# First mixer of a hybrid two-layer backbone: a fixed TensorE order for its products and recurrences

## The chip, the cores and the metric

The kernel runs on one core of a Trainium2 chip. The metric is the device time of one execution in microseconds. Before the change the median of three runs is 1795.73 us (1795.3 to 1796.77).

## The reference, cut to what matters

Two layers work on 512 latent tokens and 256 context tokens of width 1024, in float32. Layer 0 is the part that the change rewrites. One projection feeds two head groups: gated linear attention (GLA), a recurrence run in both directions, and softmax attention with grouped heads.

```python
gq, gk, gv, gog, gz, aq, ak, av = _split(h @ w_in, EVEN_SIZES)   # 256 256 512 512 32 512 128 128
for d, z in enumerate(jnp.split(gz, 2, axis=-1)):
    logit = (z @ gla_w_gate[d] + gla_b_gate[d])
    g = _heads(jax.nn.log_sigmoid(logit) / GLA_GATE_TAU, GLA_HEADS)
    dirs.append(_directional_scan(q, k, v, g, n_ctx, reverse=(d == 1)))   # context first, latent starts from its end state
a_lat = _gated_readout(dirs[0][1] + dirs[1][1], og[:, :, n_ctx:], gla_out_norm)   # rms(o) * silu(og)
...
o = scores(q, k, decay) @ v + (q * exp(G)) @ s       # one chunk of the recurrence
s = s * exp(G_last) + (k * exp(G_last - G)).T @ v
```

Then softmax attention over context and latent keys, one output projection, and a SwiGLU FFN. Layer 1 has a recurrence of the same form (HGRN2) and another FFN. Shift, scale and gate of every sub-layer come from a condition vector: `silu(c) @ mod_w`, 1024 x 6144 per layer.

## The kernel before, in words

**Products.** A float32 product is made of three passes with operands split into a high part `H` and a rest `L` (`mm3`, L476). `unit` (L461) loads 512 KB of weights on SP's queue into one of three `raw` buffers. ACT writes the high part `wH`, VectorE the rest `wL` (four buffers each). `gemm_nat` (L501) gives 256 output columns for all 768 tokens: three token pairs (4, 0, 2) of 48 matmuls each, in a `nat` tile of PSUM that ACT evacuates after each pair. `gemm_T` (L483) gives 128 output rows for all tokens, in a 512 and a 256 token group (tile `gqk`).

**The first mixer** (`even_mixer`, L809) needs these products: the gate input `z` (288 columns, with part of the attention queries), queries `q` and keys/values `kv` of attention, and for each of two head pairs `c`: `qk` (two `gemm_T`), values `v` and output gate `g`. The string on L909 is the order in which they are traced. `g1` is handed to `attention` as filler instead.

**The gates** (`gla_gates`, L937) come right after `z`: eight small `logit` products, two directions times two token ranges times two head pairs. All eight use one PSUM bank (`sc1`). ACT (L950) and VectorE (L953) both read it before the next can start. These eight stand ahead of all other products in trace order.

**A recurrence job** (`gla_job`, L959, and `scan`, L655) exists for each head pair and token range: `c0`, `l0`, `c1`, `l1` (context, latent; pairs 0 and 1). The latent job needs the end states of the context job. A job doubles the block size from 1 to 64 in seven levels. Each level has two ACT copies (L718), two VectorE products on `arr` (L723), and a small one (L724). In between, TensorE computes small score blocks: `pcg` after the first three and after all levels, then `pbg`. Then come the transposed keys `knpg`, the state sums `pdg`, a chain of state updates on VectorE (L789), and outputs `pog` (L796 to L806): per token tile one matmul with the scores (128 rows) and up to two with the states (64 rows, one head's half of the partitions). Two heads share a job, so `hpp` is 2. In layer 1 `hpp` is 1.

**Condition sums.** `mod_vec` (L313) multiplies 512 KB pieces of `mod_w` by one element per partition and adds them on VectorE (`macc`, L333 and L335). At the end come eight matmuls (`mod_acc`), a copy and transposes (`mod_cols`, L275), and for gates a further transpose (`gate_rows`, L371). It is a generator; `even_mixer` advances it five steps after each product. All of it ends before the first recurrence job, because its pool makes room for theirs.

**What sets the order.** Tile's planner orders each engine's instructions itself; in the first mixer it is free to. `pin` (L158) takes that away where `self.pinned` is set: each pinned matmul or transpose is queued behind whatever was traced just before it on TensorE. Until now only the second mixer sets it (L1293). Nothing else is pinned: VectorE, ACT and the DMA queues keep the planner's order. The line that a pinned instruction adds:

```python
def pin(self, r):
    if self.pinned:
        self.tc.keep_in_program_order(r)
    return r
```

**Attention preparation** (`att_prep`, L997) normalizes and rotates queries and keys, six token tiles one after another: a square on ACT, a reduction, a power on GpSimd, a product with `rs` on VectorE (L1029), and the rotation on VectorE. `attention` (L1040) turns keys and queries, then computes scores `S`, probabilities and values with a head start of three items.

Of the kernel before, what the change touches and what calls it, by code (L numbers as in the profile page):

```python
# [133 lines left out]
class Net:  # L134
# [140 lines left out]
    def mod_cols(self, l, acc, n, outs):  # L275

        nc = self.nc
        rows = self.wp.tile([P, WU], F32, tag="mraw", bufs=2, name="modrows")[:, :n]
        nc.vector.tensor_copy(rows, acc)
        pt = self.tr_tile("modT")  # L280
        nb = n // P
        for b in range(nb):
            last = self.tr(pt[:, b * P : (b + 1) * P], rows[:, b * P : (b + 1) * P], self.ident)
        v = pt[:, :n].rearrange("p (b j s) -> p j b s", b=nb, j=4)
        for m, r, k, j, row, nj in outs:
            kk = nb * nj
            bias = self.modb[:, l * 48 + 8 * m + k : l * 48 + 8 * m + k + kk]
            dst = self.modcol[l, m][:, r, k : k + kk]
            nc.vector.tensor_tensor(
                dst.rearrange("p (j b) -> p j b", j=nj), v[:, j : j + nj, :, row], bias.rearrange("p (j b) -> p j b", j=nj), op=ALU.add  # L290
            )
        return last

    def mod_group(self, l, ms, which=None, pool=None, bufs=2):
# [16 lines left out]
        self.mod_cols(l, acc, n, [(m, r, 0, per * i, r, per) for i, m in enumerate(ms) for r in range(2)])  # L311

    def mod_vec(self, pool, jobs, own=None, bufs=2):  # L313
# [7 lines left out]
        for l, ms, then in jobs:  # L321
            self.mod_tiles(l, [m for m, r in ms if r == 0])
            accs = [pool.tile([P, D], F32, tag="macc", bufs=2, name=f"macc{l}{m}{r}") for m, r in ms]
# [47 lines left out]
    def gate_rows(self, l, m, row, streams=2):  # L371
# [6 lines left out]
        pt = self.tr_tile(f"gcT{l}{m}")  # L378
        self.tr(pt[0:n, 0:P], gc.rearrange("p r k -> p (r k)"), self.ident)
        gt = self.wp.tile([P, WU], F32, tag="mraw", bufs=2, name=f"gt{l}{m}")[0:n, :P]  # L380
        nc.vector.tensor_copy(gt, pt[0:n, 0:P])
        self.gates[l, m] = self.dr.tile([streams, D], F32, name=f"gd{l}{m}")
        nc.scalar.dma_start(out=self.gates[l, m].rearrange("r (k p) -> (r k) p", p=P), in_=gt)
# [271 lines left out]
    def scan(self, pool, nm, arr, q, ksum, dscale, f, nt, hpp, V, first, ends, o_evac):  # L655
# [24 lines left out]
        CT = pool.tile([P, ns, 32], F32, tag="CT", bufs=2, name=f"CT{nm}")  # L680
# [27 lines left out]
        while b < P:  # L708
            qk = pool.tile([P, 2, N], F32, tag="qk", bufs=4, name=f"qk{nm}{b}")
# [21 lines left out]
        compact([(qks[x][:, 0, :], qks[x][:, 1, :], m) for m, x in ((3, 8), (4, 16))])  # L731


        ST = pool.tile([P, ns, P], F32, tag="qk" if hpp > 1 else "ST", bufs=4 if hpp > 1 else 1, name=f"ST{nm}")
# [38 lines left out]
        for d, (order, steps) in enumerate(orders):  # L773
# [10 lines left out]
            for i, t in enumerate(steps):  # L784
                S = pool.tile([P, P], F32, tag="S", bufs=10, name=f"S{nm}{d}{t}")
# [23 lines left out]
    def even_mixer(self, h, mix, zu, last):  # L809
# [92 lines left out]
        def att_q():  # L902
            self.gemm_nat(w, 1536 + 288, 256, h, tiles, ev_q)
# [796 lines left out]
```

## Time and profile before

| what | value |
|---|---|
| median of three runs | 1795.73 us |
| profiled execution | 1793.05 us |
| its span, first to last instruction | 1791.3 us |
| TensorE / VectorE / ACT busy | 97% / 73% / 48% |
| mean granted TensorE clock | 0.988 |
| first and last `logit` product start | 60.66 and 84.09 us |
| first recurrence matmul (`pcg`) | 139.7 us |
| last output matmuls (`pog`) end | 264.5 us |
| first attention score `S` | 273.4 us |

How to read it. Times are microseconds from the start of the span, unless marked ns. The page has a line of busy time per engine. A stretch row names start and end, length, then for each engine its busy time and number of instructions, the granted clock (1.00 is full speed), the share of the DMA engines and GB/s. Asked for one tile, the same row counts only instructions that read or write it. A group row has line, engine, operation, output and input tile with shapes, count, total and mean time, and the idle time before them with what ended it. A timeline row has start, length, engine, line and what it is. Matmuls are pipelined: their starts show how fast they run, their lengths overlap. A float32 matmul that is not split appears as two records.

### The profile page before, as it was taken

To read this page: it belongs to the slowest core of one execution; us is meant where nothing else is said; L and a number is where in the kernel's file an instruction comes from. 1 tells how busy PE (TensorE), PEld (TensorE's weight loads), DVE (VectorE), ACT (ScalarE), POOL (GpSimd) and SP (SyncE) were. 2 spreads that over 40 slices of the span, in tenths; PEclk is the share of its full clock that TensorE was granted. 3 is DMA by queue.
4 is the path that set the end of the run, shared out by engine and by line. 5 is a ranking of instruction groups with operands and counts; after the bars stand their busy time and mean duration, and the time that the engine had idled before them with its cause. 6 is when DMAs were issued, how large, how long until landed. Compare 5 with 4: busy or idle time off the path is not lost. (4 is left out here: it accounts for less than half of the span.)

```text
span 1791.3 us, 33164 instructions
## 1 busy us (share of the span) xinstructions
PE 1737.8 (97%) x13864; PEld 1548.3 (86%) x13864; DVE 1305.7 (73%) x2123; ACT 856.7 (48%) x1486; POOL 57.5 (3%) x73
## 2 busy tenths in 40 slices
PE   6999999999999999999999999999999999999998
PEld 4897985888998879898998998988898899999997
DVE  5857768863878999796676516878775487878885
ACT  5625446753653233333335725666663564444442
POOL 1002100000000000000000100000000000000000
PEclk8999999999999999999999999999999999999999
DMA  8641013023343456552215322112124323333333
GB/s 313 199 120 46 27 35 115 2 71 118 109 149 108 141 177 200 164 155 65 66 59 165 118 60 72 48 48 61 48 60 132 124 77 115 96 95 104 89 107 125
DMA packets 169586, 187.27 MB, mean 105 GB/s; under 512 B 6198, under 2 KB 140892, under 8 KB 169436
## 3 DMA queue, kind: packets, MB, share of 16 engines
q1 hardware_dynamic: 167504, 181.56, 32.4%
q10 hardware_dynamic: 1932, 3.59, 0.6%
q8 instruction: 109, 1.79, 0.4%
q14 instruction: 41, 0.34, 0.1%
HBM read 175.66 MB, written 9.46 MB: 103 GB/s over the span
## 5 line engine op out<-in xcount | busy, mean ns | idle before, releaser
L470 DVE TENSOR_TENSOR wL<-raw,wH 128x1024 fp32r<-128x1024 f32 (+1 forms) x126 | 151.1, 1206 | 129.6 <-ACT wH L469 129.4
L165 PE MATMUL nat<-wH,x 128*128 128x256 f32 (+1 forms) x1216 | 230.5, 288 | 1.6 <-issue 1.5
L524 ACT CAST wH<-raw 128x1024 fp32r<-128x1024 f32 x120 | 124.5, 1051 | 188.6 <-PE acc L165 64.1
L165 PEld LDWEIGHTS nat<-wH,x 128*128 128x128 f32 x1216 | 194.4, 194 | 3.0 <-issue 2.6
L525 DVE TENSOR_TENSOR wL<-raw,wH 128x1024 fp32r<-128x1024 f32 x120 | 145.2, 1220 | 65.3 <-ACT wH L524 65.1
L469 ACT CAST wH<-raw 128x1024 fp32r<-128x1024 f32 (+1 forms) x126 | 129.0, 1039 | 128.3 <-PE nat L165 36.9
L165 PE MATMUL nat<-wL,x 128*128 128x256 f32 (+1 forms) x608 | 175.3, 288 | 0.0
L165 PE MATMUL acc<-wH,gH 128*128 128x512 f32 x440 | 172.1, 391 | 0.0
L165 PE MATMUL acc<-wH,gL 128*128 128x512 f32 x440 | 171.8, 390 | 0.0
L165 PE MATMUL acc<-wL,gH 128*128 128x512 f32 x440 | 171.7, 390 | 0.0
L617 DVE TENSOR_TENSOR y<-y,acc 128x1024 f32<-128x1024 f32 x135 | 114.6, 861 | 26.9 <-PE acc L165 23.9
L165 PE MATMUL ff<-x,wH 128*128 128x512 f32 (+1 forms) x512 | 127.6, 340 | 0.0
L335 DVE SCALAR_TENSOR_TENSOR macc<-mraw,scT,macc 128x1024 f32<-128x1024 f32 x98 | 122.9, 1276 | 5.9 <-DMA mraw<-in_mod_w_dram 5.8
L165 PEld LDWEIGHTS nat<-wL,x 128*128 128x128 f32 x608 | 118.0, 194 | 3.9 <-issue 3.4
L397 POOL TENSOR_TENSOR rs<-ms,neghalf 128x1 f32<-128x1 f32 (+2 forms) x62 | 55.7, 898 | 1718.5 <-DVE ms L395 1718.5
L165 PE MATMUL oproj<-wH,x 128*128 128x512 f32 x320 | 102.8, 399 | 3.1 <-ACT x L438 3.0
L165 PEld LDWEIGHTS acc<-wH,gH 128*128 128x128 f32 x440 | 82.7, 188 | 18.8 <-issue 1.7
L165 PEld LDWEIGHTS acc<-wH,gL 128*128 128x128 f32 x440 | 82.6, 188 | 17.0
L165 PEld LDWEIGHTS acc<-wL,gH 128*128 128x128 f32 x440 | 82.7, 188 | 16.3
L165 PEld LDWEIGHTS ff<-x,wH 128*128 128x128 f32 x512 | 87.3, 190 | 10.0
L718 ACT COPY qkh<-arr 128x512 f32<-128x512 f32 x112 | 70.1, 642 | 36.3 <-DVE arr L723 32.1
L165 PE MATMUL ff<-x,wL 128*128 128x256 f32 (+1 forms) x256 | 86.2, 337 | 0.0
(328 smaller groups left out, 4143.2 us busy)
## 6 DMA issues: line engine op xcount, KB each, us to landing
mraw<-in_mod_w_dram SPq DMA_DIRECT2D x96, 512.0 KB, 4.5
raw<-in_ffn_w_gate_dram SPq DMA_DIRECT2D x44, 512.0 KB, 3.8
raw<-in_ffn_w_up_dram SPq DMA_DIRECT2D x44, 512.0 KB, 3.8
raw<-in_ffn_w_down_dram SPq DMA_DIRECT2D x44, 512.0 KB, 3.7
raw<-in_odd_w_in_dram SPq DMA_DIRECT2D x40, 512.0 KB, 3.7
raw<-in_even_w_in_dram SPq DMA_DIRECT2D x16, 512.0 KB, 4.8
x<-xr SPq DMA_DIRECT2D x14, 512.0 KB, 2.7
xr<-x SPq DMA_DIRECT2D x14, 512.0 KB, 3.2
```

The lines of the kernel that those rows point to most:

```text
L165: return self.pin(self.nc.tensor.matmul(*a, **k))
L335: nc.vector.scalar_tensor_tensor(a, u, w, a, op0=ALU.mult, op1=ALU.add)
L397: nc.gpsimd.tensor_tensor(rs, ms, self.neghalf.to_broadcast([P, w]), op=ALU.pow)
L469: nc.scalar.copy(H[:, :m], raw[:, :m])
L470: nc.vector.tensor_tensor(L[:, :m], raw[:, :m], H[:, :m].bitcast(F32), op=ALU.subtract)
L524: self.nc.scalar.copy(H, f)
L525: self.nc.vector.tensor_tensor(L, f, H.bitcast(F32), op=ALU.subtract)
L617: nc.vector.tensor_tensor(y, y, pt, op=ALU.add)
L718: nc.scalar.copy(qkv[:, :, :, half, :], dst)
```

## The change

`even_mixer` sets `self.pinned` and walks through two written orders. Every product, recurrence job, the condition sums (`m`) and attention preparation (`p`) become generators. A name in the string advances that piece by one step: the first step of a product only loads weights, each further one is a token pair (or, for `qk`, a token group). The order lets `c0` and `l0` run side by side, later `c1` and `l1`. `g1` moves out of attention into the mixer. Buffers are cut per job size (`arr256`, `arr512`, `qk256`, `qk512`, one `CT`).

Outputs of a job are issued by kind: first all score matmuls of both heads (`start` only on the first of a bank), then the state matmuls, alternating between heads. Some work moves from VectorE to ACT: the `arr` copies, two of four block copies for `hpp` 2, and the product with `rs` in attention preparation, which becomes one ACT instruction per head. `macc` has four buffers in the first mixer. `mod_vec` pauses between its matmuls and the transposes that follow, also where it runs inside the first FFN. `scan` has one more pause; the second mixer advances it twice there.

```diff
@@ mod_vec
-    def mod_vec(self, pool, jobs, own=None, bufs=2):
+    def mod_vec(self, pool, jobs, own=None, bufs=2, sums=2):
...
-            self.mod_cols(l, acc, 512, [(m, r, 0, 2 * n, 0, 2) for n, (m, r) in enumerate(ms)])
+            turned = self.mod_cols(l, acc, 512, [(m, r, 0, 2 * n, 0, 2) for n, (m, r) in enumerate(ms)])
+            yield
+            turned()
             if then:
-                self.gate_rows(l, *then)
+                rows = self.gate_rows(l, *then)
+                yield
+                rows()
@@ scan
-        CT = pool.tile([P, ns, 32], F32, tag="CT", bufs=2, name=f"CT{nm}")
+        CT = pool.tile([P, ns, 32], F32, tag="CT", bufs=1 if hpp > 1 else 2, name=f"CT{nm}")
...
-            qk = pool.tile([P, 2, N], F32, tag="qk", bufs=4, name=f"qk{nm}{b}")
+            qk = pool.tile([P, 2, N], F32, tag=f"qk{N}", bufs=4 if N > CTX else 3, name=f"qk{nm}{b}")
...
         compact([(qks[x][:, 0, :], qks[x][:, 1, :], m) for m, x in ((3, 8), (4, 16))])
+        yield
...
-            nc.vector.tensor_copy(ST[ps_, :, 32 * j : 32 * j + 32], CT[ps_, :, :])
+            (nc.vector.tensor_copy if j % 2 or hpp == 1 else nc.scalar.copy)(ST[ps_, :, 32 * j : 32 * j + 32], CT[ps_, :, :])
...
-        for hh, t0, n in groups:
-            po = self.tr_tile(f"po{nm}").rearrange("p (s v) -> p s v", s=4)
+        pos = [self.tr_tile(f"po{nm}").rearrange("p (s v) -> p s v", s=4) for _ in groups]
+        terms = {t: [(S[t], a) for S, a in zip(states, (3, 1)) if t in S] for t in range(nt)}
+        for po, (hh, t0, n) in zip(pos, groups):
             for t in range(t0, t0 + n):
-                terms = [(ST[:, hh * nt + t, :], V(t, hh))]
-                for d, a in ((0, 3), (1, 1)):
-                    S = states[d].get(t)
-                    if S is not None:
-                        terms.append((arr[rowp(hh), a, t * P : (t + 1) * P], S[rowp(hh), :]))
-                for i, (l, r) in enumerate(terms):
-                    self.mm(po[:, t - t0, :], l, r, start=(i == 0), stop=(i == len(terms) - 1))
+                self.mm(
+                    po[:, t - t0, :], ST[:, hh * nt + t, :], V(t, hh), start=t == t0, stop=not terms[t], skip_group_check=True
+                )
+        for i in range(4):
+            for x in range(2):
+                for po, (hh, t0, n) in zip(pos, groups):
+                    if i >= n or x >= len(terms[t0 + i]):
+                        continue
+                    S, a = terms[t0 + i][x]
+                    tok = slice((t0 + i) * P, (t0 + i + 1) * P)
+                    self.mm(
+                        po[:, i, :], arr[rowp(hh), a, tok], S[rowp(hh), :], start=False, stop=x == len(terms[t0 + i]) - 1,
+                        skip_group_check=True,
+                    )
+        for po, (hh, t0, n) in zip(pos, groups):
             o_evac(hh, t0, n, po[:, :n, :])
@@ even_mixer
-        mods = self.mod_vec(tp, ((0, ((2, 0), (2, 1)), (2, R_NQM)), (0, ((3, 0), (3, 1)), None)), tp, 3)
+        mods = self.mod_vec(tp, ((0, ((2, 0), (2, 1)), (2, R_NQM)), (0, ((3, 0), (3, 1)), None)), tp, 3, 4)
+
+        def nat(c0, evac):
+
+            us = self.nat_units(w, c0, 256, 0) + self.nat_units(w, c0, 256, 1)
+            yield
+            for t0 in tiles:
+                self.gemm_nat(w, c0, 256, h, (t0,), evac, us=us)
+                yield
...
-        for step in "q kv qk0 v0 c0 prep l0 qk1 v1 g0 c1 r0 l1".split():
...
+        def run(steps):
+            for x in steps.split():
+                if x not in running:
+                    running[x] = kinds[x]()
+                next(running[x], None)
+
+        self.pinned = True
+        run("qk0 qk0 m m m v0 qk0 m m qk0 m m qk0 m m q v0 m m m v0 m m m v0 m m m kv q m m m q m m m q m m m qk1 kv m m m kv m m m")
+        for _ in mods:
+            pass
+        tp.release()
+        gp = self.open_pool("gla")
+        run("c0 l0 kv c0 v1 qk1 c0 qk1 qk1 c0 l0 qk1 c0 c1 v1 c0 l0 g0 v1 l0 p v1 l0 c1 p p g0 l0 c1 l1 g1 p g0 c1 p g0 c1 l1 p p")
+        run("g1 c1 l1 g1 l1 l1 r0 r0 r0 g1 l1")
         gp.release()
         mg.__exit__(None, None, None)
-
+        self.pinned = False
...
-            self.attention(ap, natq, natk, heads_done, lambda: gates(1), {i: (lambda t=t: readout(1, (t,))) for i, t in zip((18, 20, 22), tiles)})
+            self.attention(ap, natq, natk, heads_done, lambda: None, {i: (lambda t=t: readout(1, (t,))) for i, t in zip((18, 20, 22), tiles)})
@@ gla_job
-        arr = gp.tile([P, 4, N], F32, tag="arr", bufs=2, name=f"arr{nm}")
+        arr = gp.tile([P, 4, N], F32, tag=f"arr{N}", bufs=1, name=f"arr{nm}")
         q, k = gq[:, tok], gk[:, tok]
-        nc.vector.tensor_copy(arr[:, 0, :], k)
-        nc.vector.tensor_copy(arr[:, 2, :], k)
+        nc.scalar.copy(arr[:, 0, :], k)
+        nc.scalar.copy(arr[:, 2, :], k)
@@ att_prep
         for i, t in enumerate((4, 5, 0, 1, 2, 3)):
+            yield
...
-                nc.vector.tensor_tensor(x, x, rs[:, hs][:, :, None].to_broadcast([P, n, 64]), op=ALU.mult)
+                for j in range(n):
+                    nc.scalar.activation(x[:, j, :], x[:, j, :], AF.Identity, scale=rs[:, hs.start + j : hs.start + j + 1])
@@ odd_mixer
-                go(scan)
+                go(scan, scan)
```

More of the change, by code (lines that the diff above doesn't have):

```diff
@@ L279, in mod_cols, with turned @@
         nc.vector.tensor_copy(rows, acc)
[L280 to L292, printed above, removed]
+        def turned():
+            pt = self.tr_tile("modT")
+            nb = n // P
+            for b in range(nb):
+                last = self.tr(pt[:, b * P : (b + 1) * P], rows[:, b * P : (b + 1) * P], self.ident)
+            v = pt[:, :n].rearrange("p (b j s) -> p j b s", b=nb, j=4)
+            for m, r, k, j, row, nj in outs:
+                kk = nb * nj
+                bias = self.modb[:, l * 48 + 8 * m + k : l * 48 + 8 * m + k + kk]
+                dst = self.modcol[l, m][:, r, k : k + kk]
+                nc.vector.tensor_tensor(
+                    dst.rearrange("p (j b) -> p j b", j=nj),
+                    v[:, j : j + nj, :, row],
+                    bias.rearrange("p (j b) -> p j b", j=nj),
+                    op=ALU.add,
+                )
+            return last
+        return turned
     def mod_group(self, l, ms, which=None, pool=None, bufs=2):
@@ L310, in mod_group @@
                 )
[L311 to L313 removed]
+        self.mod_cols(l, acc, n, [(m, r, 0, per * i, r, per) for i, m in enumerate(ms) for r in range(2)])()
+    def mod_vec(self, pool, jobs, own=None, bufs=2, sums=2):
         nc = self.nc
@@ L322, in mod_vec @@
             self.mod_tiles(l, [m for m, r in ms if r == 0])
-            accs = [pool.tile([P, D], F32, tag="macc", bufs=2, name=f"macc{l}{m}{r}") for m, r in ms]
+            accs = [pool.tile([P, D], F32, tag="macc", bufs=sums, name=f"macc{l}{m}{r}") for m, r in ms]
             while i < len(steps) and steps[i][0] == l and steps[i][2] in [m for m, _ in ms]:
@@ L377, in gate_rows, with rows @@
         nc.vector.tensor_tensor(gc, self.mod_m(l, m)[:, :streams], gain[:, None, :].to_broadcast([P, streams, 8]), op=ALU.mult)
[L378 to L383, printed above, removed]
+        def rows():
+            pt = self.tr_tile(f"gcT{l}{m}")
+            self.tr(pt[0:n, 0:P], gc.rearrange("p r k -> p (r k)"), self.ident)
+            gt = self.wp.tile([P, WU], F32, tag="mraw", bufs=2, name=f"gt{l}{m}")[0:n, :P]
+            nc.vector.tensor_copy(gt, pt[0:n, 0:P])
+            self.gates[l, m] = self.dr.tile([streams, D], F32, name=f"gd{l}{m}")
+            nc.scalar.dma_start(out=self.gates[l, m].rearrange("r (k p) -> (r k) p", p=P), in_=gt)
+        return rows
     def gate_row(self, pool, l, m, r):
@@ L885, in eo @@
                 nc.scalar.activation(og[c][:, t0 : t0 + 2, :], pt[:, :, :256], AF.Silu)
-            self.gemm_nat(w, 1024 + 256 * c, 256, h, tiles, eo)
+            return nat(1024 + 256 * c, eo)
         def readout(c, tiles=tiles):
@@ L957, in gla_gates, with gla_job @@
         return fs
-    def gla_job(self, gp, c, t0, nt, f, gq, gk, gv, states):
+    def gla_job(self, gp, c, t0, nt, f, gq, gk, gv, first, ends):
         nc = self.nc
@@ L976, in evac @@
             nc.scalar.copy(gv[:, t0 + t : t0 + t + n, (2 * c + hh) * P : (2 * c + hh + 1) * P], po)
-        ends = [] if t0 >= LT else None
-        for _ in self.scan(gp, nm, arr, q, k, 2.0, f, nt, 2, V, states, ends, evac):
-            pass
-        return ends
+        return self.scan(gp, nm, arr, q, k, 2.0, f, nt, 2, V, first, ends, evac)
     def gated_T(self, pool, src, nh, grow, cat, groups):
@@ L1527, in run @@
                         )
-                last = self.mod_cols(0, acc, 256, [(m, r, 4 * half, 2 * m, r, 2) for m in range(2) for r in range(2)])
+                last = self.mod_cols(0, acc, 256, [(m, r, 4 * half, 2 * m, r, 2) for m in range(2) for r in range(2)])()
                 gain = self.col[:, R_NPM + 4 * half : R_NPM + 4 * half + 4]
```

58 lines of the change are left out of this document (28 added, 30 removed).

## The prediction

> **What bounds the kernel now.** The page comes first: TensorE is busy nearly everywhere, and no other engine is near.
>
> ```profile
> span 1791.3 us, 33164 instructions
> PE 1737.8 (97%) x13864; PEld 1548.3 (86%) x13864; DVE 1305.7 (73%) x2123; ACT 856.7 (48%) x1486; POOL 57.5 (3%) x73
> ```
>
> The change sits in the first mixer, so the second view is the table of stretches: from the last `z` product (59.0 us) to the first recurrence, from there to the first attention score `S` (273.4), and attention up to the output projection (388).
>
> ```profile
> 59.00:138.80 79.80, 79.06 (x564) 70.21 (x566) 51.31 (x62) 32.12 (x54) 0.00 (x0) 1.00 0.47 139
> 138.80:273.40 134.60, 130.08 (x2122) 113.00 (x2123) 102.53 (x275) 64.89 (x134) 19.54 (x12) 0.95 0.14 43
> 273.40:388.00 114.60, 110.78 (x939) 84.02 (x938) 88.95 (x190) 79.52 (x187) 0.27 (x1) 0.97 0.11 38
> ```
>
> The columns are the length, then the busy time of PE, weight load, VectorE, ScalarE and GpSimd, the granted clock, and DMA. The order of the planner leaves PE only 5 us unoccupied over 214.4 us. "Busy" hides slow matmuls, however, so the third view asks the same two stretches tile by tile: `nat` (first and second stretch), `gqk` (both), `logit` (first), then, in the second, `pog`, `pcg`, `pbg`, `pdg`, `knpg`.
>
> ```profile
> 59.00:138.80 79.80, 54.49 (x432) 52.34 (x431) 5.37 (x10) 1.00 0.47 139
> 138.80:273.40 134.60, 58.15 (x432) 55.11 (x432) 5.30 (x9) 0.95 0.14 43
> 59.00:138.80 79.80, 17.35 (x96) 14.66 (x96) 0.00 (x0) 1.60 (x2) 1.00 0.47 139
> 138.80:273.40 134.60, 25.84 (x288) 18.33 (x288) 6.83 (x16) 1.61 (x2) 0.95 0.14 43
> 59.00:138.80 79.80, 7.23 (x16) 2.34 (x16) 4.90 (x8) 4.66 (x8) 1.00 0.47 139
> 138.80:273.40 134.60, 23.25 (x128) 16.95 (x128) 3.82 (x8) 0.95 0.14 43
> 138.80:273.40 134.60, 15.02 (x1152) 12.48 (x1152) 9.05 (x40) 1.96 (x8) 0.95 0.14 43
> 138.80:273.40 134.60, 6.16 (x192) 5.47 (x192) 3.85 (x8) 0.95 0.14 43
> 138.80:273.40 134.60, 5.25 (x80) 4.26 (x80) 6.28 (x20) 0.95 0.14 43
> 138.80:273.40 134.60, 3.28 (x20) 2.10 (x20) 3.17 (x8) 0.95 0.14 43
> ```
>
> The 96 `gqk` records cost 17.35 in the first stretch, and some 5 us more in the second, where they are cut up among recurrence steps (its row also holds 192 small `pcg` records that read `gqk`). Undisturbed `nat`, and an output block whose 24 matmuls all use 128 rows (`poh`, second layer), run faster than the same kinds in the second stretch:
>
> ```profile
> 198.00:222.00 24.00, 24.00 (x202) 24.00 (x201) 2.35 (x4) 1.00 0.06 19
> 1322.46:1325.31 2.85, 2.84 (x24) 2.65 (x24) 0.00 (x0) 1.00 0.18 42
> ```
>
> That is 0.119 us per `nat` and 0.119 per output record, against 0.135 (58.15/432) and 0.182 (23.25/128).
>
> **The change part by part.** I rebuild the way from 59.0 to the first `S` under the new order and compare it with 214.4.
>
> *Start of the fixed order.* A pinned matmul queues behind the matmul traced just before it. The first pinned one belongs to `qk0`; before it stands the last of eight `logit` products, which are not pinned and share one PSUM bank. So no product can run until the eighth logit is issued. Today products fill that chain:
>
> ```profile
> 60.66 0.67 PE L165 MATMUL logit<-zT,wg 32*128 32x256 f32 x2 [0.27 <-issue]
> 84.09 1.12 PE L165 MATMUL logit<-zT,wg 32*128 32x512 f32 x2
> L950 ACT ACTIVATE am<-logit,col 128x512 f32<-128x512 f32 x4 | 2.8, 691 | 3.5 <-PE logit L165 3.5
> L950 ACT ACTIVATE am<-logit,col 128x256 f32<-128x256 f32 x4 | 1.9, 474 | 2.7 <-PE logit L165 2.7
> L953 DVE TENSOR_SCALAR am<-logit,col 128x512 f32<-128x512 f32 x4 | 3.0, 746 | 0.3 <-ACT am L950 0.3
> L953 DVE TENSOR_SCALAR am<-logit,col 128x256 f32<-128x256 f32 x4 | 1.9, 480 | 2.0 <-ACT am L950 1.9
> L335 DVE SCALAR_TENSOR_TENSOR macc<-mraw,scT,macc 128x1024 f32<-128x1024 f32 x24 | 29.9, 1271 | 0.0
> ```
>
> Per logit the bank is held for PE, then ACT, then VectorE: 4 x (0.67 + 0.47 + 0.48) + 4 x (1.12 + 0.69 + 0.75) = 16.7 us. Without the last one's 1.44 of reading, the eighth ends at 60.66 + 15.3 = 76.0 at the earliest. Now it ends at 85.2. I take 81: VectorE still slips 1.27 us `macc` updates in front of bank reads, and ACT its weight casts and a table load. 81 - 59 = **22.0 us** before the first product, of which PE works 7. All six products of `nat`, all `gqk` products and both recurrence inputs queue behind it. VectorE, which is not pinned, goes on with `macc`, so the condition sums are early rather than late.
>
> *Clock there.* PE would be busy about a third of that time. Low activity costs clock in this trace even without a long gap:
>
> ```profile
> 150.00:175.00 25.00, 23.68 (x412) 19.09 (x414) 20.27 (x55) 11.40 (x26) 6.23 (x3) 0.86 0.15 44
> 225.00:250.00 25.00, 22.43 (x589) 20.15 (x587) 21.18 (x64) 13.81 (x33) 1.50 (x1) 0.86 0.16 46
> ```
>
> 0.86 over 25 us is 7 us at half speed, with 1.3 us of idle PE in all. I charge **2.0** (half of some 4 us in which the first products run slow); bounds 0 and 9, the latter if the logits' 7.2 us of PE time doubles too. The Trainium skill ("TensorE: Matmul & The Clock Gate", section "HAM oscillation — how this bites in real kernels") asks only for no idle gap over about 3.4 us. By that rule the sum would hold 0 here, since a logit comes every 2 to 3 us; the first row contradicts it.
>
> *Products in pieces.* Same matmuls, other places. Whole blocks of 48 run undisturbed: 864 x 0.119 = **102.8** (now 112.6), and 2 x 17.35 = **34.7** for `gqk`. Upper bound: today's costs, 15 more. The two weight loads of `g1` (512 KB each) move ahead on SP's queue, into stretches with a DMA share of 0.14; that hides them.
>
> *Recurrences.* `pcg`, `pbg`, `pdg`, `knpg` stay: 15.0 + 6.2 + 5.3 + 3.3 = 29.8. I take **27.5**, since some of it ran at half clock.
>
> *Outputs by kind.* 48 of the 128 `pog` records use 128 rows and 80 use 64 rows. Now each token tile switches twice; then there is one switch per job. At the `poh` rate this is 128 x 0.119 = 15.2. The 64-row records will alternate between two halves of the array and two banks. The nearest row that alternates halves is `pdg`, 5.25/80 = 0.066: 48 x 0.119 + 80 x 0.066 = 11.0. I take **12.0**, nearer the row that alternates. In the second layer the same reordering changes only 128-row records: nothing.
>
> *Condition sums.* Two sums of eight matmuls, whose transposes now wait in a fixed queue for a copy:
>
> ```profile
> 102.97 1.06 PE L165 MATMUL mod_acc<-macc,one 128*32 128x512 f32 x8
> L279 DVE COPY modrows<-mod_acc x2: 684/688/692, 104.7 to 139.8; 128x512 f32<-128x512 f32 x2
> ```
>
> 2 x 1.06 plus transposes, and about one copy with its small additions: **4.0**. Four accumulators let the second sum start early; by 81 us that matters little. The extra pauses also shift the later condition sums among FFN blocks; no instruction is added, and FFN products cover them: 0, bounds +-2.
>
> *Engines that feed the stages.* Moved from VectorE to ACT: the scaling in attention preparation, the `arr` copies, half of the block copies.
>
> ```profile
> L1029 DVE TENSOR_TENSOR natq<-natq,rs 128x512 f32<-128x512 f32 x6 | 4.2, 693 | 7.8 <-POOL rs L397 7.8
> L1029 DVE TENSOR_TENSOR natk<-natk,rs 128x128 f32<-128x128 f32 x6 | 1.7, 285 | 0.0
> L1025 ACT ACTIVATE rope<-natq 128x512 f32<-128x512 f32 x6 | 3.8, 632 | 0.0
> L1025 ACT ACTIVATE rope<-natk 128x128 f32<-128x128 f32 x6 | 1.9, 309 | 0.1
> L754 ACT COPY STg<-pbg 128x512 f32<-128x512 f32 x4 | 2.3, 586 | 5.7 <-PE pbg L165 5.7
> L769 ACT COPY kng<-knpg 128x384 f32<-128x384 f32 x4 | 1.8, 488 | 0.0
> L789 DVE SCALAR_TENSOR_TENSOR Sg<-Sg,glaf,pdg 128x128 f32<-128x128 f32 x16 | 5.3, 342 | 0.2
> ```
>
> The scaling leaves VectorE 5.9 us lighter. On ACT it becomes 60 instructions of 64 columns; the two L1025 rows give 0.84 ns per column, so 0.255 us each, 15 us. With the copies ACT's 65 in the second stretch becomes about 87, and VectorE's 102.5 about 92. PE's own work there is one `nat` third, three `nat` products and a `gqk` pair (5.7 + 51.4 + 17.4) plus 39.5 for recurrences: 114. PE stays the longest. But in a fixed order it stands still when a stage is not ready. Stages without a product between them: the last latent job's states behind its own block copies (0.59 + about 0.5 + 0.49, some 2.5 with hand-overs); compactions behind banks that the state updates still read (4 x 0.34 once, half of it once, plus queueing: 3); the rest 2.5. Sum **8.0**; bounds 3 and 20.
>
> *Start of attention.* Today the rest of `g1` runs over it: keys are turned at 264.5, the first score comes at 273.4.
>
> ```profile
> 264.47 0.44 PE L168 MATMUL kT<-ident,natk 128*128 128x128 f32 x2
> 269.51 0.63 PE L168 MATMUL qT<-ident,natq 128*128 128x128 f32 x4 [0.29 <-DVE qs L1076]
> 273.44 0.28 PE L165 MATMUL S<-kH,qs 128*128 128x256 f32 x1
> ```
>
> That cover is gone: after the last output block PE waits for keys and queries, which were ready about when the second `qT` ran, 5 us after `kT`: **5.0**. In return ACT and VectorE have no `g1` work at that point: **-2.0**.
>
> Sum: 22.0 + 2.0 + 102.8 + 34.7 + 27.5 + 12.0 + 4.0 + 8.0 + 5.0 - 2.0 = 216.0, against 214.4: **+1.6 us**. The profiled execution took 1793.05 (its span is 1791.3, 1.75 lies outside); its answer would be 1794.7. The median of the three runs is 1795.73, 2.7 higher, so I predict **1797 us**: the faster order pays for the stretch it leaves open.
>
> **Rivals.** (1) *The logits cost little*: the chain runs at its minimum (76.0) with full clock, and the stages wait for 3 us only. That takes 5 + 2 + 5 off: 1785. For it: VectorE and ACT are half idle there. Against it: in the trace L953 regularly starts behind a `macc`. (2) *The order is not fixed there at all*, because the planner gets products in between the logits: 22.0 becomes 7.2, the 2.0 vanishes: 1780. For it: only matmuls traced after the switch are pinned. Against it: those are all the products there are. (3) *The recurrences become the bound*: slower. One latent job's level needs an ACT copy and two VectorE products in turn, and two jobs plus attention preparation now share both in-order engines. It decides once a stage comes later than the product placed before it, 5.7 us, lasts. At four waits of 3 us beyond my 8, 1809; with the clock bound (+7), 1816. For it: VectorE needs 92 of some 125 us and ACT 87, in alternation. Against it: the first jobs' opening levels can run long before PE reaches them.
>
> On outputs, the Trainium skill ("TensorEngine Tiling (Array Packing)", section "Theoretical Speedup") lets two 64-row tiles work at once. By it 80 records would cost as much as 40, the term would be 10.5 and the sum 1.5 lower; in `pog` the trace of before shows no such pair.
>
> **How the numbers follow.** A change under 0.2% (3.6 us) can't be told from none here. Forecast 0.45 (own range 1790 to 1804), rival 1 0.18, rival 2 0.12, rival 3 0.25. Within the forecast I give 0.16 to faster than 1792.1, 0.50 to the band, 0.34 to above 1799.3: faster 0.07 + 0.30 = 0.37; same 0.23 + 0.03 (the low end of rival 3) = 0.26; slower 0.15 + 0.22 = 0.37. The range leaves out most of rival 2 and the far half of rival 3: 1783 to 1811.
>
> **What would show it.** Right: between the `z` products and the first `gqk` only `logit` matmuls, until 76 to 87 us, at a lower clock; six `nat` products at about 0.12 us a record; `pog` near 12 us instead of 23; a pause of PE between the last `pog` and the first `S`, which falls near 275. Wrong: products between logits (rival 2), or PE waiting over 15 us in all on `pcg`, `pbg` and `pdg` (rival 3). The prediction fails if the first `S` comes before 266 or after 284, or if attention or a later stage changes by more than 4 us.

## The result, and the profile after

The changed kernel is slower: 1812.52 us (median of 4 runs, 1809.26 to 1817.93) against 1795.51 for the kernel before beside it, a ratio of 1.0097 with an interval of 1.0072 to 1.0122. Run once more on another chip it took 1808.59 against 1792.87, ratio 1.0084 (1.0067 to 1.0101). Predicted were 1797 us and a range up to 1811.

The page of the changed kernel: the span grew from 1791.3 to 1810.8, and TensorE is occupied for less of it although it issues the same 13864 instructions. The clock row falls to 6 in its second slice (45 to 91 us) and to 8 from the fifth to the seventh (181 to 317), where before it has 9.

```profile
span 1810.8 us, 33217 instructions
PE 1728.3 (95%) x13864; PEld 1547.5 (85%) x13864; DVE 1299.4 (72%) x2095; ACT 877.4 (48%) x1562; POOL 59.1 (3%) x73
...
PEclk8699888999999999999999999999999999999999
```

The stretches of the changed kernel, cut where its phases now end: last `z` product, first product, first recurrence, first score.

```profile
59.00:85.50 26.50, 12.86 (x20) 3.72 (x18) 23.88 (x32) 16.62 (x32) 0.00 (x0) 0.58 0.57 178
85.50:161.60 76.10, 74.65 (x558) 69.74 (x558) 44.35 (x67) 32.74 (x68) 3.89 (x2) 0.97 0.30 87
161.60:296.00 134.40, 117.08 (x2108) 109.66 (x2107) 77.70 (x202) 67.53 (x162) 15.24 (x8) 0.90 0.14 41
296.00:410.00 114.00, 107.92 (x932) 82.89 (x933) 90.13 (x197) 79.22 (x187) 2.01 (x2) 0.94 0.13 38
```

In the first one TensorE works 12.86 of 26.5 us, at a clock of 0.58. In the third it stands still for 17.3 us, while VectorE is occupied for 77.70 of 134.4 and ACT for 67.53. Neither is a bottleneck by load. The same TensorE stretches by tile, as in the prediction: `nat` (second and third stretch), `gqk` (both), then in the third `pog`, `pcg`, `pbg`, `pdg`, `knpg`.

```profile
85.50:161.60 76.10, 52.69 (x432) 0.97 0.30 87
161.60:296.00 134.40, 57.70 (x433) 0.90 0.14 41
85.50:161.60 76.10, 19.35 (x100) 0.97 0.30 87
161.60:296.00 134.40, 24.73 (x288) 0.90 0.14 41
161.60:296.00 134.40, 11.27 (x128) 0.90 0.14 41
161.60:296.00 134.40, 14.46 (x1152) 0.90 0.14 41
161.60:296.00 134.40, 5.77 (x192) 0.90 0.14 41
161.60:296.00 134.40, 5.47 (x80) 0.90 0.14 41
161.60:296.00 134.40, 3.06 (x20) 0.90 0.14 41
```

Outputs by kind did their part, 11.27 instead of 23.25. The products did not get cheaper: `nat` 110.4 instead of 112.6. The groups of `logit`, `gqk` and `S` (count, shortest, median and longest in ns, first and last start) date the phases:

```profile
L165 PE MATMUL logit<-zT,wg x16: 374/924/1217, 61.4 to 84.5; 32*128 32x256 f32 x8, 32*128 32x512 f32 x8
L165 PE MATMUL gqk<-x,wH x128: 278/389/795, 85.5 to 192.9; 128*128 128x512 f32 x64, 128*128 128x256 f32 x64
L165 PE MATMUL S<-kH,qs x80: 277/386/582, 296.0 to 399.3; 128*128 128x256 f32 x48, 128*128 128x512 f32 x32
```

No product runs until the eighth logit is out, and the first score comes at 296.0 instead of 273.4. TensorE's waits between 59 and 300 us (sum, times, longest):

```profile
PE logit L165 <- DVE am L998: 11.8, 7, 2.5
PE pcg L165 <- DVE Sg L805: 6.0, 3, 3.9
PE pcg L165 <- issue: 5.9, 3, 2.9
...
PE pcg L165 <- ACT qkg L733: 1.2, 1, 1.2
...
PE pcg L165 <- DVE CTg L720: 1.1, 1, 1.1
...
PE pdg L165 <- ACT kng L785: 0.6, 2, 0.3
```

The timeline shows one of the places where a recurrence stands still: the state sums of `l0` are issued, and the next instruction in the fixed queue is the first compaction of `c1`, whose banks the state updates (L805) still read. Nothing stands between the two.

```profile
217.39 1.53 PE L165 MATMUL pdg<-gvo,kng 128*64 128x128 f32 x24
220.69 0.30 PE L165 MATMUL pcg<-gqk,gqk 64*32 64x32 f32 x13 [1.77 <-DVE Sg L805]
...
225.32 0.32 PE L165 MATMUL pcg<-qkg 64*32 64x32 f32 x3 [2.89 <-issue]
```

One later stretch got shorter. From the first `acc` (first layer's FFN) to the first `ff` (a product of the second mixer) it is 556.2 us (533.6 to 1089.8) instead of 560.2. So the first mixer lost some 23 us and the FFN gave back 4, in this profile.

### The profile page after: what moved, and what is told of

The parts are those of the page before. It is cut to its first block, busy times and chain, and to the rows that moved or that the text cites. A ratio compares the mean times of both kernels' runs of the same rounds, so it can differ in the third digit from the quotient of the medians.

```text
span 1810.8 us, 33217 instructions
## 1 busy us (share of the span) xinstructions
PE 1728.3 (95%) x13864; PEld 1547.5 (85%) x13864; DVE 1299.4 (72%) x2095; ACT 877.4 (48%) x1562; POOL 59.1 (3%) x73
## 5 line engine op out<-in xcount | busy, mean ns | idle before, releaser
L632 DVE TENSOR_TENSOR y<-y,acc 128x1024 f32<-128x1024 f32 x135 | 114.8, 862 | 30.6 <-PE acc L165 27.3
```

The source lines that it names most:

```text
L632: nc.vector.tensor_tensor(y, y, pt, op=ALU.add)
```

## The experiments

The theory after the result: the loss has two parts, the chain of logits in front of the first pinned product, and compactions in the fixed order with nothing to run while their banks are read. The rival: the recurrences, or the work moved to ACT, are too slow by themselves. All runs in one table; "before" is the kernel before on the same chip, "S" the first score, "FFN" the way from the first `acc` to the first `ff`, both from the trace. Times are medians; where two kernels ran on different chips, compare their ratios.

| run | us | before | ratio (interval) | S | FFN |
|---|---|---|---|---|---|
| before | 1795.51 | | | 273.4 | 560.2 |
| changed | 1812.52 | 1795.51 | 1.0097 (1.0072 to 1.0122) | 296.0 | 556.2 |
| changed again | 1808.59 | 1792.87 | 1.0084 (1.0067 to 1.0101) | 295.6 | 552.4 |
| first phase free | 1789.72 | 1793.22 | 0.9982 (0.9972 to 0.9991) | 274.7 | 553.4 |
| product before two compactions | 1804.42 | 1793.22 | 1.0071 (1.0053 to 1.0089) | 292.1 | 553.3 |
| both | 1784.32 | 1793.22 | 0.9956 (0.9939 to 0.9973) | 271.4 | 552.9 |
| before + outputs by kind | 1786.98 | 1793.22 | 0.9959 (0.9942 to 0.9977) | 263.8 | 561.2 |
| before + kinds + pauses | 1779.53 | 1794.93 | 0.9926 (0.9908 to 0.9943) | 264.8 | 552.8 |
| changed, moves to ACT undone | 1804.71 | 1794.93 | 1.0057 (1.0041 to 1.0073) | 292.0 | 553.4 |
| logits on two banks | 1804.76 | 1794.93 | 1.0062 (1.0041 to 1.0083) | 288.0 | 553.6 |
| extra light matmuls | 1807.93 | 1794.93 | 1.0078 (1.0059 to 1.0097) | 295.4 | 552.4 |
| changed, never pinned | 1782.45 | 1794.04 | 0.9936 (0.9918 to 0.9954) | 265.2 | 556.8 |
| never pinned, moves undone | 1779.57 | 1794.04 | 0.9926 (0.9912 to 0.9939) | 265.4 | 554.2 |
| both, moves undone | 1780.35 | 1794.04 | 0.9932 (0.9916 to 0.9948) | 266.1 | 553.8 |
| before + kinds + pauses + moves | 1780.11 | 1794.04 | 0.9932 (0.9914 to 0.9949) | 264.3 | 553.7 |
| extra dense matmuls | 1806.39 | 1792.87 | 1.0072 (1.0055 to 1.0089) | 291.7 | 553.2 |
| scaling back on VectorE | 1805.60 | 1792.87 | 1.0064 (1.0048 to 1.0081) | 289.0 | 553.4 |
| copies back on VectorE | 1806.31 | 1792.87 | 1.0070 (1.0054 to 1.0086) | 293.5 | 554.5 |

**The first phase free.**

```diff
-        self.pinned = True
         run("qk0 qk0 m m m v0 qk0 m m qk0 m m qk0 m m q v0 m m m v0 m m m v0 m m m kv q m m m q m m m q m m m qk1 kv m m m kv m m m")
...
         gp = self.open_pool("gla")
+        self.pinned = True
         run("c0 l0 kv c0 v1 qk1 c0 qk1 qk1 c0 l0 qk1 c0 c1 v1 c0 l0 g0 v1 l0 p v1 l0 c1 p p g0 l0 c1 l1 g1 p g0 c1 p g0 c1 l1 p p")
```

> The order is pinned only from the second written string on (c0 l0 ...); the products before it are free again, everything else is as after the change. Theory (the eight logits, left without products, cost 85.5 - 59 - 7 = 19 us of TensorE): products run between the logits again, the first qk0 product no longer waits for 85.5, the first attention score moves from 296 to about 279, median 1796 (1793 to 1800). Rival (the recurrences are bound by VectorE and ACT, so an earlier start only waits longer later): first score after 290, median 1806 to 1813.

Measured 1789.72, a ratio below 1 (faster than the theory's 1793 to 1800). Products start at 59.4 and run among the logits:

```profile
59.00:85.00 26.00, 25.78 (x128) 18.12 (x126) 23.65 (x32) 18.52 (x35) 0.00 (x0) 1.00 0.63 183
```

TensorE is occupied all through, at full clock. The first score comes 21.3 us earlier than in the changed kernel. So pinning the products behind the logits is worth more than the whole loss. The run frees the whole first string and not that place alone, but behind the first product TensorE works 74.65 of 76.10 us in the changed kernel, so little else can be lost there.

**A product in front of two compactions.** In the strings one step of a product moves ahead of the first compaction of `c1` and of `l1`.

```diff
-        run("c0 l0 kv c0 v1 qk1 c0 qk1 qk1 c0 l0 qk1 c0 c1 v1 c0 l0 g0 v1 l0 p v1 l0 c1 p p g0 l0 c1 l1 g1 p g0 c1 p g0 c1 l1 p p")
-        run("g1 c1 l1 g1 l1 l1 r0 r0 r0 g1 l1")
+        run("c0 l0 kv c0 v1 qk1 c0 qk1 qk1 c0 l0 qk1 c0 c1 v1 c0 l0 g0 v1 l0 p v1 l0 p p g0 c1 l0 c1 l1 g1 p g0 c1 p g0 c1 p p")
+        run("g1 l1 c1 l1 g1 l1 l1 r0 r0 r0 g1 l1")
```

> Pinned as after the change, but the first compaction of c1 and of l1 stands behind one more product (g0 and g1), not directly behind the state sums of the other job. Theory (the compaction waits for two PSUM banks that state updates still read, 1.8 + 3.9 us, and for what follows from it, with the clock at half for 17 us around these two places): waits on pcg in the first mixer fall from 14 us to under 7, half-clock time after 160 us falls by 10 us or more, median 1804 (1800 to 1808). Rival (VectorE and ACT are late at these stages whatever stands before): the waits appear at the next stage, median 1810 to 1815.

> Both edits: pinned from the second string on, and one more product before the first compaction of c1 and of l1. Theory (two separate losses): the gains add, 16 + 8, median 1788 (1783 to 1794), faster than both kernels. Rival (VectorE and ACT bound the recurrences): 1800 or more.

1804.42 and 1784.32: both times are inside the theory's ranges. For the first of them that shows little, since its ratio's interval overlaps with the changed kernel's; but the four runs of the second (1782.59 to 1785.85) all lie below those of the first phase free (1787.04 and more). The waits did not do what the theory said: on `pcg` they were to fall from 14 us to under 7, and fell from 14.2 to 11.0. Between 215 and 265 us, this kernel's waits on `pcg` first, then the changed kernel's:

```profile
PE pcg L165 <- DVE CTg L720: 2.6, 2, 1.9
PE pcg L165 <- DVE Sg L805: 2.5, 1, 2.5
PE pcg L165 <- issue: 1.4, 1, 1.4
```

```profile
PE pcg L165 <- DVE Sg L805: 6.0, 3, 3.9
PE pcg L165 <- issue: 4.2, 2, 2.9
```

10.2 us became 6.5. The wait is not gone, part of it moved to the mask copies (L720) of the same compactions. The first score comes 3.9 us earlier (3.3 with the first phase free, where the medians show 5.4).

**Outputs by kind alone**, on the kernel before; the diff is that of `scan`'s last part.

> The kernel before the change, free order, with nothing but the outputs by kind (all score matmuls first, then the state matmuls of both heads in turn). Theory (each change between 128-row and 64-row matmuls costs about 0.2 us, and TensorE bounds this stretch): pog falls from 23 us to 11 to 15, median 1787 (1784 to 1791). Rival (the planner covers the outputs, or takes the blocks apart again): pog falls, the time stays within 2 us of 1795.5.

1786.98, as the theory had it: this part alone gains 0.4%, `pog` occupies TensorE for 12.09 us instead of 23.25, and the first score comes at 263.8 against 273.4.

**With the pauses of the condition sums.** `mod_vec`, `mod_cols` and `gate_rows` as changed, nothing else.

> The kernel before (order free) with two parts of the change alone: outputs by kind (1786.98 by itself) and the pauses of the condition sums (mod_vec, mod_cols, gate_rows). Theory: in the changed kernel the way from the first down-projection matmul (acc, 533.6) to the second layer's ff (1089.8) is 556 us against 560 before, 553 with the two early repairs and 561 with outputs by kind alone, because the pauses give the copies behind a sum one block of products to finish. Then the pauses alone bring that way to 553 to 557 here, and the time to 1780 (1776 to 1784). Rival: the way is shorter because the sums of the first mixer stand elsewhere, and not for the pauses: the way stays at 560 or more, and the time within 3 us of 1787.

1779.53, the FFN way 552.8. So the pauses alone make the later gain, and the rival falls. The reason that I gave is not what the trace points to. One stretch of the FFN with about the same 190 matmuls, in the kernel before, with TensorE's longest waits there and ACT's for the casts:

```profile
616.90:659.80 42.90, 38.63 (x193) 33.35 (x192) 40.35 (x47) 12.22 (x17) 0.00 (x0) 0.96 0.52 163
...
L335 DVE SCALAR_TENSOR_TENSOR macc<-mraw,scT,macc 128x1024 f32<-128x1024 f32 x14 | 17.3, 1278 | 0.4 <-DMA mraw<-in_mod_w_dram 0.4
...
PE E L165 <- ACT wH L524: 2.0, 1, 2.0
PE E L165 <- DVE y L617: 1.0, 1, 1.0
...
ACT wH L524 <- DVE raw L549: 2.4, 2, 1.9
```

and in this one:

```profile
608.10:642.70 34.60, 34.09 (x188) 32.16 (x185) 33.84 (x42) 11.22 (x17) 0.00 (x0) 1.00 0.53 159
...
L342 DVE SCALAR_TENSOR_TENSOR macc<-mraw,scT,macc 128x1024 f32<-128x1024 f32 x11 | 13.7, 1277 | 0.0
```

VectorE is nearly full in both, and it splits the weights that TensorE needs. The pauses shift the sums by steps, so three additions of 1.28 us and the eight matmuls of a sum (2.1 us) fall outside this stretch, and it takes 8.3 us less. TensorE stands still for 0.5 us of it instead of 4.3, and the clock (0.96, which is 3.4 us at half speed) gives up to 1.7. The longest waits are for weights and for `y`, which VectorE prepares, and none is for the copy behind a sum. By these rows VectorE's load is what TensorE waits for there; no run moved the additions by themselves.

**Moves to ACT undone**, all three and one by one, with the changed kernel again beside the last two.

```diff
-        nc.scalar.copy(arr[:, 0, :], k)
+        nc.vector.tensor_copy(arr[:, 0, :], k)
...
-                for j in range(n):
-                    nc.scalar.activation(x[:, j, :], x[:, j, :], AF.Identity, scale=rs[:, hs.start + j : hs.start + j + 1])
+                nc.vector.tensor_tensor(x, x, rs[:, hs][:, :, None].to_broadcast([P, n, 64]), op=ALU.mult)
```

> The changed kernel with the three moves from VectorE to ACT undone (arr copies, block copies, scaling in attention preparation). Theory: TensorE waits at the compactions because the state updates that free the banks stand behind other work on VectorE; giving VectorE 5.9 us of scaling and the copies back lengthens that queue, so the time is the same or worse, 1812 to 1818. Rival: the 60 small ACT instructions and the copies delay the ACT copies that the recurrence levels need, and this is what the fixed order pays for: 1804 to 1809.

> The changed kernel with one of the three moves undone: the scaling of attention preparation is back on VectorE. Theory: on ACT the first scaling instruction waits for GpSimd's power (5.2 us in two waits from 140 to 180), and the copies of the recurrence levels stand behind it on ACT; the two pauses of TensorE at the compaction after 168 follow from that. This move alone makes up what undoing all three gained: 5 to 8 us faster than the changed kernel in this call, the pauses at 168 gone. Rival: the arr and block copies do it: within 2 us of the changed kernel.

> The changed kernel with the other two moves undone (arr copies and block copies back on VectorE), the scaling left on ACT. Theory: within 2 us of the changed kernel in this call. Rival: 5 to 8 us faster than it.

> The changed kernel once more, beside the two above on one chip, since 8 us between kernels of two calls is little more than their intervals. Theory: 1809 to 1814. Rival, if the 8 us were a difference of chips: 1803 to 1808.

The first theory (1812 to 1818) was wrong: 1804.71 lies in its rival's range. It looked like a gain of 8; beside the changed kernel's 1808.59 it is 4 (5 by ratio), and the changed kernel came out just under its theory's 1809 to 1814. The scaling gives 3.0, where its theory had 5 to 8, and the copies 2.3, where theirs had up to 2. Both are within what the intervals leave open, so the times alone do not decide. The trace shows the mechanism that the theory of the scaling named. ACT's waits between 140 and 180 us in the changed kernel, then with the scaling back:

```profile
ACT natq L1073 <- POOL rs L412: 5.2, 2, 3.7
ACT natk L893 <- PE nat L165: 4.2, 1, 4.2
...
ACT qkg L733 <- DVE arrg L738: 0.3, 1, 0.3
```

```profile
ACT natk L893 <- PE nat L165: 7.2, 3, 4.2
ACT qkg L733 <- DVE arrg L738: 5.2, 4, 4.2
```

The wait on GpSimd's power is gone. With it goes most of two pauses of TensorE at the compaction behind 168: 1.1 and 1.2 us in the changed kernel and with the copies back, 0.3 in all here and with all three moves undone. The fall of the clock from 172.5 to 176.0 goes as well, and the first score comes at 289.0 instead of 295.6. The pauses make 2.0 of these 6.6 us and the clock up to 1.7; the medians show 3.0. The largest wait at a compaction, 3.9 us before 256 in the changed kernel, is 4.7 us before 249 here. The scaling itself occupies ACT for 16.5 us, where the prediction had 15.

**Logits on two banks.**

```diff
-                pt = self.sc_tile(f"logit{c}{d}", 1)[:, :N]
+                pt = self.sc_tile(f"logit{c}{d}", d)[:, :N]
```

> The changed kernel with the eight logits on two PSUM banks in turn, so that a logit does not wait for ACT and VectorE to read the one before it, but the one before that. Theory: the chain in front of the first product is the single bank's; ACT has four instructions for each logit, some 17 us in all, and becomes the next limit. First gqk at 75 to 81 instead of 85.5, time 1803 to 1808. Rival: ACT's order or the halved clock sets the pace already: first gqk at 83 or later, time 1809 to 1814.

1804.76, the first product at 77.3 instead of 85.5, TensorE's wait on the reads of the logits 6.8 us instead of 11.8. The first score comes 8 us earlier, at 288.0, as the theory had it; the ratio falls by 0.2 to 0.35%, 4 to 6 us, though its interval overlaps with the changed kernel's. So by the trace the single bank set the chain's pace, and a part of the loss can be had back without touching the order.

**Extra matmuls behind each logit.**

```diff
+                for _ in range(2):
+                    self.mm(fill[:, :256], self.ident, self.scT.rearrange("p k r -> p (k r)"), start=True, stop=True)
```

> The changed kernel with two extra matmuls (128 rows, 256 columns, written to a bank that nobody reads) queued behind each logit, which keep TensorE occupied while it would stand still; nothing is left out. Theory: TensorE's clock is halved from 63.3 to 90.6 because it does little there; logits at half clock (924 ns a record instead of 532) are part of the chain. With the extra matmuls the clock stays at 1.00, the logit records return to some 530 ns, the first gqk comes at 77 to 81 and the first products run at full clock: 1804 to 1808. Rival: the clock falls for another reason, or the logits' own length is not what the chain waits for: the first gqk stays at 84 to 87, time 1811 to 1815.

In the second form four matmuls of split activations, 128 rows by 512 columns.

> The changed kernel with four extra matmuls of the products' own kind behind each logit (128 rows, 512 columns, split activations as both operands; a bank that nobody reads). The earlier extra matmuls (plain float32, mostly zero columns) occupied TensorE and did not bring the clock back before 91.0. Theory: those were too light for whatever the clock follows; with the products' kind it returns to 1.00 before the last logit, logit records near 530 ns, first gqk at 79 to 84, time 1802 to 1808. Rival: the clock's fall has nothing to do with how much TensorE does at that time; it stays at 0.50 until 89 to 91 again, and the time at 1806 to 1813.

1807.93 and 1806.39, against 1812.52 and 1808.59: no effect that can be told. In the second form TensorE has no idle time left behind the first logit (before it, 1.2 us), but look at the clock (first the changed kernel, then the second form):

```profile
70.00:77.00 7.00, 4.00 (x6) 1.49 (x6) 5.83 (x8) 5.14 (x10) 0.00 (x0) 0.50 0.39 137
77.00:85.00 8.00, 4.05 (x6) 0.99 (x4) 7.45 (x10) 5.44 (x10) 0.00 (x0) 0.50 0.43 131
```

```profile
70.00:77.00 7.00, 7.00 (x13) 3.25 (x12) 5.08 (x7) 4.43 (x9) 0.00 (x0) 0.50 0.39 138
77.00:85.00 8.00, 8.00 (x15) 3.67 (x14) 7.10 (x10) 5.80 (x12) 0.00 (x0) 0.50 0.42 124
```

It stays at 0.50. The rival holds: occupying TensorE with these matmuls does not bring the clock back. The logits stayed at 924 ns, and the first product came at 87.9 and 89.1.

**Never pinned in the first mixer**, all else as changed.

```diff
-        self.pinned = True
         run("qk0 qk0 m m m v0 qk0 m m qk0 m m qk0 m m q v0 m m m v0 m m m v0 m m m kv q m m m q m m m q m m m qk1 kv m m m kv m m m")
```

> The changed kernel with its order written but not fixed: pinned is never set in the first mixer, all else stays (pieces, strings, two recurrences side by side, outputs by kind, moves, accumulators, pauses). Theory: what the change loses is the fixed order alone (logits without products among them some 22 us, stages that come late some 8 to 11 us), so it gives 1777 to 1786, beside 1779.53 for outputs by kind and pauses on the old trace order. Rival: two recurrences side by side, the smaller buffers or the moves to ACT lose time by themselves: 1788 or more.

> The same with the three moves to ACT undone too. In the fixed order undoing them gave 1804.71 against 1812.52. Theory: they delay ACT copies that a fixed order then waits for; where the planner can put other products in between they cost nothing: within 3 us of the unfixed kernel with the moves. Rival: they cost time whatever the order: 4 to 9 us faster than it.

> The fixed order with the first phase free and one product in front of each of two compactions (1784.32 before), with the three moves to ACT undone. Theory: the moves delayed the stages of the fixed order, as in the changed kernel: 1777 to 1781. Rival: the 8 us that undoing them gained there was a wait that these two repairs remove already: 1782 to 1787.

> Outputs by kind and pauses on the old, unfixed order (1779.53) with the three moves to ACT alone added. Theory: ACT is half idle and TensorE has other products to run, so they cost nothing: 1778 to 1782. Rival: they delay the levels of the recurrences, the last of which nothing covers: 1783 to 1789.

1782.45, 1779.57, 1780.35, 1780.11: all four inside their theories' ranges. Without the fixed order the changed kernel is faster than the kernel before, as the theory said. The moves cost 2.9 us there, inside the first theory's 3 us and below the rival's 4; on the old order, by ratio, 1 us. With both early repairs undoing them brings 4, as the theory for that run had it, though 1784.32 came from another chip. These four and the 1779.53 can't be told apart: their intervals overlap. None beats outputs by kind and pauses on the old order, which leaves the largest part of the change out.

Put in a row by ratio: outputs by kind 0.9959; with the pauses 0.9926; with pieces, two recurrences under way, buffers and moves but no pinning 0.9936; with the second phase pinned 0.9982; with the first one too 1.0084 to 1.0097. The two pinnings cost 0.5% and 1.0 to 1.2%, 8 and about 20 us.

## Why the prediction was wrong, step by step

The sign of the sum was right, its size was not. With +1.6 us and the same chance, 0.37, for faster and for slower, the sign was luck. The way from 59.0 to the first score was predicted at 216.0 us and is 237.0: the first score comes at 296.0, where 284 was named as the end of what the prediction allows. Time from one matmul's start to the next, put down to the first one's kind:

| term | predicted | measured |
|---|---|---|
| until the first product | 22.0 | 26.5 |
| `nat` and `gqk`, with 2.0 for the clock | 139.5 | 109.0 + 41.2 = 150.2 |
| `pcg`, `pbg`, `pdg`, `knpg`, and 8.0 of waits | 35.5 | 41.0 |
| outputs by kind | 12.0 | 11.7 |
| condition sums | 4.0 | 4.5 |
| start of attention | 3.0 | 3.0 |

*Start of the fixed order: right, 4.5 short.* Only logits run until 85.5, inside 76 to 87. It is where it was said, and the largest single loss. Rival 2 (not fixed there) is out, and rival 1 (logits cost little) too.

*Products in pieces and the clock: the step that failed most, by 10.7.* I let blocks of 48 run undisturbed at 0.119 us a record, because they do so in an even stretch of the kernel before. They ran at 0.126 (109.0/864), hardly below the 112.8 of before by the same count, and `gqk` at 41.2 instead of 34.7. The clock accounts for most of it. In the trace's record it has two values, 1.00 and 0.50. Behind the first product the changed kernel runs 33.0 us at 0.50 until the first score (5.1 up to 90.6 us, 27.9 in five later stretches), the kernel before 13.7 on the same way. `nat` and `gqk` have 21.8 of the 33.0 (8.2 and 13.6), which can cost them up to 10.9. My 2.0 covered only the first products. The rest of the dips lie in the recurrences, and not in the pinned kernels alone: the kernel that is never pinned has 0.90 between 160 and 275 as well.

```profile
160.00:275.00 115.00, 102.64 (x1846) 95.33 (x1846) 75.28 (x191) 62.97 (x141) 11.80 (x8) 0.90 0.18 50
```

Other kernels that are not pinned have 0.93 there (moves undone as well) and 0.94 to 0.99 (old order, with outputs by kind and pauses, without and with the moves), each from one profile, so no run shows whether two recurrences side by side bring it. What the traces do show is what stands before a fall in these two kernels: a stretch of 3.4 us in which TensorE is occupied for little, whether by one long wait or by several short ones.

```profile
59.85:63.26 3.41, 0.81 (x3) 0.44 (x4) 3.31 (x7) 1.15 (x4) 0.00 (x0) 1.00 0.88 281
251.10:254.50 3.40, 1.32 (x19) 0.94 (x17) 3.37 (x11) 3.40 (x12) 0.00 (x0) 1.00 0.00 0
```

Before the six falls from 60 to 296 us of the changed kernel it is occupied for 0.81, 1.65, 2.10, 1.46, 1.32 and 1.45 us of 3.4; before the three of the never pinned kernel for 1.45, 0.54 and 1.51. The edge is not sharp: two such stretches of the changed kernel with 1.95 and 2.02 us (from 111.1 and 216.9) brought no fall, and in the kernel before one fall, at 238.8, follows 2.96 of 3.4. By these rows waits of stages cost twice, once as idle time and once more by the clock behind them. The sum priced the second only behind the logits.

*Waits of stages: the place right, 5.5 short.* I gave compactions "behind banks that the state updates still read" 3 us. They took 6.0, and the pauses marked "issue" within the same bursts 5.9. All waits on `pcg` and `pdg` make 14.8, just under the 15 by which rival 3 was to be told. Its price came true (1809, or 1816 with the clock), its reason only in part. The loads moved about as predicted: from 59 us to the first score VectorE is occupied for 145.9 us instead of 153.8 and ACT for 116.9 instead of 97.0 (10.5 less and 22 more were expected). But part of the work is done before 161.6 us, so in the stretch of the recurrences they need 77.7 and 67.5 of 134.4, not 92 and 87 of 125: neither sets the pace by its load. Stages come late, and at these places there was no product in front of them. The strings showed that, and I priced it by the updates' own 0.34 us instead of by the queue in front of them. Before the 3.9 us wait the state sums start at 251.32, and VectorE, whose order the planner keeps, first finishes rotations of attention preparation (L1080 to L1082):

```profile
254.25 0.68 DVE L1082 TENSOR_TENSOR natq<-natq,rope 128x512 f32<-128x512 f32 x1
254.85 0.28 DVE L1082 TENSOR_TENSOR natk<-natk,rope 128x128 f32<-128x128 f32 x1
255.05 0.28 DVE L803 COPY Sg<-pdg 128x128 f32<-128x128 f32 x1
```

No run moved these rotations. Not all such waits are the fixed order's either: the never pinned kernel has 7.0 us of them on `pcg` (3.2 for the state updates, 3.8 "issue").

*Outputs by kind: right.* 11.7 against 12.0. The first job's group shows why; eight records with 128 rows and eight with 64:

```profile
L165 PE MATMUL pog<-gvo,STg x8: 273/275/275, 200.1 to 200.9; 128*128 128x128 f32 x8
L165 PE MATMUL pog<-Sg,arrg x8: 272/272/373, 201.1 to 201.6; 64*128 64x128 f32 x8
```

0.11 us from start to start, then 0.07 on average. The single starts show pairs: the second of two 64-row matmuls starts 0.007 us behind the first, the next pair 0.105 later, so a pair takes the 0.112 of one 128-row matmul; a change of kind takes 0.2. The Trainium skill ("TensorEngine Tiling (Array Packing)", section "Theoretical Speedup") gives up to twice the rate for 64 rows, and inside these pairs the trace agrees. The prediction said that the trace of before shows no such pair; it has a few (eight starts of 0.006 to 0.014 us among its 80 records), but most stand 0.11 to 0.21 apart.

*Later stages: wrong.* I put the shifted condition sums at nothing, bounds 2 either way. They gain about 8 us of FFN (561.2 to 552.8 on the old order; in the first profile of the changed kernel 4, in the second 8; the two part at one place near 815 us, where the first has waits of 2.9 us instead of 1.2 and 3.4 us at half clock). This hid part of the loss. That FFN products cover the sums is what I assumed; by the rows of the FFN stretch VectorE carries both, and where it is full a sum in another place is worth microseconds.

## What to carry to other kernels

Before an order is fixed, look at what is queued just ahead of the first fixed instruction: here eight small matmuls on one bank kept all products back for 26 us that a free order had filled. In a fixed order, price a stage that reuses a bank by the queue of the engine that frees the bank, not by the last instruction in it, and put a product in front of it; here one product before each of two such stages gave 5.4 us, and did not end the waits. And take a mixed change apart: two small parts of this one gain 0.7%, and fixing the order turns that into a loss of 0.8 to 1.0%.

## What the runs showed of the hardware

By the trace's record of it, the granted clock fell to half at 62.0 to 63.8 us in every kernel that ran the eight logits ahead of the products on one bank, and came back at 89.3 to 91.1, also where extra matmuls kept TensorE occupied from 66 us on or earlier. With two banks, where the last logit matmul starts at 76.3, it fell at 65.4 and came back at 82.5. The Trainium skill ("TensorE: Matmul & The Clock Gate", sections "HAM oscillation — how this bites in real kernels" and "Part 1: The HAM clock gate (the "warmup" mystery)") lets it fall after an idle gap of over about 3.4 us and return after about as much sustained work. Neither agrees here: the longest wait on the logits' reads was 2.5 us, and with the dense extra matmuls 7.00 of 7.00 us of work ran at 0.50. Most falls follow 3.4 us of low occupation, as shown above, and each stretch at 0.50 between 60 and 1400 us lasts a whole multiple of 3.4 us in every trace (3.4, 6.8, 10.2, 13.7, 17.1 or 27.3); what brings the clock back stays open. What those stretches from 62 to 90 have in common is the logits, matmuls with 32 of 128 rows. Logits alone do not hold the clock down: in the kernel before and with the first phase free, where products run among the same eight, it is 1.00 from 59 to 85 us.

The pauses marked "issue" (5.9 us in three) all lie within bursts of `pcg` matmuls that start 0.009 us apart on average at full clock (two in the bursts of 256, one in a burst of 128), and 16 KB transfers on the queue of instructions fall beside them, at 184.25, 223.13 and 257.94 us. That TensorE waits there for its own instructions is an inference; no run tests it.
